# Loads reordered on one queue, and the first tile's multiplies divided differently: a dense expert dispatch on one core

## The chip, the cores and the metric

The kernel runs on one core of a Trainium2 chip. The metric is the device time of one execution in microseconds (us), median of three runs. The profile is of one further execution, taken by the hardware profiler; its times count from the first instruction of the kernel, so its span is somewhat shorter than the device time.

The engines that occur here are VectorE (DVE in the profile), ScalarE (ACT), SyncE (SP, which here only issues transfers) and the core's 16 DMA engines, which move data between HBM and the on-chip memory. "SPq" and "ACTq" are the instruction queues of SP and ACT, from which transfers are issued.

## The reference

For each of 2048 tokens, eight gate weights are normalized by their sum, and the token's 512 values are multiplied by each of the eight:

```python
def setup_inputs():
    batch, seq_len, d_model, n_experts = 8, 256, 512, 8
    # x: (8, 256, 512) float32, gate_weights: (8, 256, 8) float32
def reference(x, gate_weights):
    gate_weights = gate_weights / (np.sum(gate_weights, axis=-1, keepdims=True) + 1e-8)
    output = x[:, :, None, :] * gate_weights[:, :, :, None]
    return output.astype(np.float32)          # (8, 256, 8, 512)
```

4.2 MB of x and 64 KB of gates are read, and 33.6 MB are written.

## The kernel before

The 2048 tokens are laid on 128 partitions with 16 tokens each. Below, "token j" means the j-th token of every partition: one step that handles token j handles 128 tokens of the batch. Its output, eight experts by 512 values, is 4096 values for each partition.

All inputs are loaded by three transfers, which are moved ahead of the barrier at the kernel's entry, so that they are issued first of all. x is loaded in two parts, `HEAD` = 4 tokens and then the other twelve, from SP's queue; the gates from ACT's queue.

```python
SLOTS = 10
HEAD = 4
CHUNKS = ((0, 2, 0), (2, 3, 2), (5, 3, 5), (8, 4, 0), (12, 4, 6))   # first token, tokens, first slot
# ...
    g_all = pool.tile([P, J, E], fp32)
    x_all = pool.tile([P, J, D], fp32)
    ring = pool.tile([P, SLOTS, E, D], fp32)
# ...
    first_load = nc.sync.dma_start(out=x_all[:, 0:HEAD, :], in_=x_v[:, 0:HEAD, :])
    gate_load = nc.scalar.dma_start(out=g_all, in_=g_v)
    last_load = nc.sync.dma_start(out=x_all[:, HEAD:J, :], in_=x_v[:, HEAD:J, :])
    issue_before_entry_barrier(nc, [first_load, gate_load, last_load])

    nc.vector.memset(warm, 0.0)
    nc.scalar.copy(out=warm, in_=warm)          # brings ACT's table load forward
```

Then VectorE normalizes all gates in four operations (lines 74 to 77):

```python
    nc.vector.reduce_sum(out=gsum, in_=g_all, axis=mybir.AxisListType.X)
    nc.vector.tensor_scalar_add(out=gsum, in0=gsum, scalar1=1e-8)
    nc.vector.reciprocal(out=gsum, in_=gsum)
    nc.vector.tensor_tensor(
        out=gn, in0=g_all, in1=gsum.to_broadcast([P, J, E]), op=mult
    )
```

The output is made in a ring of ten slots, one slot for each token. There are two forms of the multiply: a small one, for one token and one expert (512 values for each partition), on ACT (line 84) or VectorE (line 86), and a broadcast one on VectorE, which makes all eight experts of a token in one operation (line 89):

```python
    def scale_one(engine, j, e, slot):
        o_ap, s_ap = ring[:, slot, e, :], gn[:, j, e : e + 1]
        if engine is nc.scalar:
            nc.scalar.mul(out=o_ap, in_=x_all[:, j, :], mul=s_ap)
        else:
            nc.vector.tensor_scalar_mul(out=o_ap, in0=x_all[:, j, :], scalar1=s_ap)

    def scale_token(j, slot):
        nc.vector.tensor_tensor(
            out=ring[:, slot, :, :],
            in0=x_all[:, j : j + 1, :].to_broadcast([P, E, D]),
            in1=gn[:, j, :].unsqueeze(2).to_broadcast([P, E, D]),
            op=mult,
        )
```

Five chunks of 2, 3, 3, 4 and 4 tokens are made and stored by one transfer each, from SP's queue. A chunk and its part of the ring are called a tile below; the first tile is tokens 0 and 1. Each of these two tokens has three small multiplies on ACT and five on VectorE.

```python
    for j0, m, s0 in CHUNKS:
        for i in range(m):
            j, slot = j0 + i, s0 + i
            if j < 2:
                for e in range(E):
                    on_act = e < 3
                    scale_one(nc.scalar if on_act else nc.vector, j, e, slot)
            elif j == 2:
                for e in range(E):
                    scale_one(nc.scalar, j, e, slot)
            elif j == 3:
                for e in range(E):
                    scale_one(nc.scalar if e < 2 else nc.vector, j, e, slot)
            elif i == 0:
                for e in range(E):
                    scale_one(nc.scalar, j, e, slot)
            else:
                scale_token(j, slot)
        nc.sync.dma_start(
            out=out_v[:, j0 : j0 + m, :, :], in_=ring[:, s0 : s0 + m, :, :]
        )
```

The fourth and fifth chunks use slots again, so their multiplies wait until earlier stores have read them.

Of the kernel before, what the change touches and what calls it, by code (L numbers as in the profile page):

```python
# [1 line left out]

# [4 lines left out]

SLOTS = 10
HEAD = 4
CHUNKS = ((0, 2, 0), (2, 3, 2), (5, 3, 5), (8, 4, 0), (12, 4, 6))  # L10


def issue_before_entry_barrier(nc, loads):
    names = [bi.ins.name for bi in loads]

    def move(nc):
        blocks = nc.main_func.blocks
        entry = blocks[0].instructions
        moved = []
        for block in blocks[1:]:  # L20
            for ins in list(block.instructions):
                if ins.name in names:
                    block.instructions.remove(ins)
                    moved.append(ins)
        assert sorted(i.name for i in moved) == sorted(names)
        for ins in reversed(moved):
            at = next(k for k, other in enumerate(entry) if other.engine == ins.engine)
            entry.insert(at, ins)

    nc.at_finalize(move)  # L30


@with_exitstack
def kernel(
    ctx: ExitStack,
    tc: tile.TileContext,
    x: bass.AP,
    gate_weights: bass.AP,
    out: bass.AP,
):  # L40
    nc = tc.nc
    P = 128

    B, S, D = x.shape
    E = gate_weights.shape[-1]
    J = B * S // P

    fp32 = mybir.dt.float32
    mult = mybir.AluOpType.mult

    x_v = x.flatten_outer_dims().rearrange("(p j) d -> p j d", p=P)
    g_v = gate_weights.flatten_outer_dims().rearrange("(p j) e -> p j e", p=P)
    out_v = out.rearrange("b s e d -> (b s) e d").rearrange(
        "(p j) e d -> p j e d", p=P
    )

    pool = ctx.enter_context(tc.tile_pool(name="pool", bufs=1))
# [4 lines that stand above are left out]
    gsum = pool.tile([P, J, 1], fp32)  # L62
    gn = pool.tile([P, J, E], fp32)
    warm = pool.tile([P, 1], fp32)

    first_load = nc.sync.dma_start(out=x_all[:, 0:HEAD, :], in_=x_v[:, 0:HEAD, :])
    gate_load = nc.scalar.dma_start(out=g_all, in_=g_v)
    last_load = nc.sync.dma_start(out=x_all[:, HEAD:J, :], in_=x_v[:, HEAD:J, :])
    issue_before_entry_barrier(nc, [first_load, gate_load, last_load])

    nc.vector.memset(warm, 0.0)  # L71
    nc.scalar.copy(out=warm, in_=warm)  # L72
# [23 lines that stand above are left out]
    for j0, m, s0 in CHUNKS:  # L96
        for i in range(m):
            j, slot = j0 + i, s0 + i
            if j < 2:
                for e in range(E):  # L100
                    on_act = e < 3
                    scale_one(nc.scalar if on_act else nc.vector, j, e, slot)
            elif j == 2:
                for e in range(E):
                    scale_one(nc.scalar, j, e, slot)
# [13 lines that stand above are left out]
# [1 line left out]
_INS = ['x', 'gate_weights']  # L120
_OUTS = [((8, 256, 8, 512), 'float32')]


# [23 lines left out]
```

## Time and profile before

| | us |
|---|---|
| device time, median of three runs (lowest, highest) | 92.21 (92.19, 92.32) |
| span of the profiled execution | 90.4 |
| VectorE busy | 46.6 |
| ScalarE busy | 26.3 |
| gates: issue, landing | 0.12, 5.13 |
| first four tokens of x: issue, issue to landing | 0.00, 4.9 |
| other twelve tokens of x: issue, issue to landing | 0.43, 11.8 |
| first multiply on ACT and on VectorE | 6.30 |
| first store issued | 10.44 |
| last store issued | 56.08 |

A transfer has two times in the profile: the issuing instruction's (some 0.4 us on SP's or ACT's queue) and the landing, when its completion reaches the engine that waits for it. Between them lies the work of the 16 DMA engines, which is shown as their mean busy share and as packets by queue: q1 is SP's queue, q10 ACT's. Mean durations of operations that follow each other on one engine overlap a little: a small multiply on VectorE is listed with 484 ns, and ten of them in a row end 4.06 us after the first begins.

### The profile page before, as it was taken

The page shows a single profiled execution, that of the slowest core. Times are in us where ns is not written, and L with a number is a line of the kernel's source. Part 1 is how long each engine was busy: PE and PEld are TensorE (multiplying, and loading weights), DVE is VectorE, ACT ScalarE, POOL GpSimd, SP SyncE. Part 2 cuts the span into 40 slices and gives each one's busy share as a digit, 9 for nine tenths or more (in the row PEclk, how much of TensorE's full clock was granted, in tenths as well). Part 3 has the DMA queues.
Part 4 walks back from the last instruction along what each step waited for, and adds up shares of the span by engine and source line. Part 5 has one row for each costly group of instructions (what it writes and reads, how often), then busy time and mean ns, then how long its engine had stood idle before and what let it go on. Part 6 is the DMA issues. An engine that isn't in the chain of part 4 may idle for free.

```text
span 90.4 us, 139 instructions
## 1 busy us (share of the span) xinstructions
DVE 46.6 (52%) x30; ACT 26.3 (29%) x42; POOL 0.2 (0%) x4
## 2 busy tenths in 40 slices
DVE  0069999999999999999990495000000000000000
ACT  4229999995990000000000497000000000000000
POOL 0000000000000000000000000000000000000000
DMA  5989899998998899888988999999999994799990
GB/s 145 511 359 511 359 464 464 464 464 348 478 565 348 348 413 630 348 348 370 674 348 348 464 464 464 464 464 464 464 464 464 464 406 203 319 464 464 464 464 0
DMA packets 1152, 37.81 MB, mean 418 GB/s; under 512 B 128, under 2 KB 256, under 8 KB 256
## 3 DMA queue, kind: packets, MB, share of 16 engines
q1 hardware_dynamic: 1008, 37.75, 97.0%
q10 hardware_dynamic: 144, 0.07, 0.3%
HBM read 4.26 MB, written 33.55 MB: 418 GB/s over the span
## 4 chain that ended last, share of the span: by engine, by line
DMA 46%; ACT 9%; DVE 6%; ACTq 1%; issue 0%; SPq 0%
DMA out_dram<-ring 41%; ACT ring L84 9%; DMA g_all<-in_gate_weights_dram 6%; DVE ring L86 4%; ACTq L142 1%; DVE gn L77 0%; DVE gsum L74 0%; DVE gsum L76 0%; DVE gsum L75 0%; ACTq L84 0%; SPq L114 0%
## 5 line engine op out<-in xcount | busy, mean ns | idle before, releaser
L89 DVE TENSOR_TENSOR ring<-x_all,gn 128x4096 f32<-128x4096 f32 x9 | 39.2, 4426 | 3.6 <-DMA out_dram<-ring 3.6
L84 ACT ACTIVATE ring<-x_all,gn 128x512 f32<-128x512 f32 x40 | 24.8, 708 | 28.5 <-DMA out_dram<-ring 24.9
L86 DVE TENSOR_SCALAR ring<-x_all,gn 128x512 f32<-128x512 f32 x16 | 6.4, 484 | 0.0
L74 DVE TENSOR_REDUCE gsum<-g_all 128x16 f32<-128x128 f32 x1 | 0.3, 286 | 3.8 <-DMA g_all<-in_gate_weights_dram 3.8
L72 ACT ACT_TABLE_LOAD x1 | 1.3, 1283 | 1.3 <-PEq L131 1.3
L71 DVE MEMSET warm<- 128x1 f32 x1 | 0.1, 59 | 1.3 <-PEq L131 1.3
L77 DVE TENSOR_TENSOR gn<-g_all,gsum 128x128 f32<-128x128 f32 x1 | 0.3, 291 | 0.0
L76 DVE RECIPROCAL gsum<-gsum 128x16 f32<-128x16 f32 x1 | 0.3, 253 | 0.0
L72 ACT COPY warm<-warm 128x1 f32<-128x1 f32 x1 | 0.2, 192 | 0.0
L75 DVE TENSOR_SCALAR gsum<-gsum 128x16 f32<-128x16 f32 x1 | 0.2, 174 | 0.0
L131 POOL MEMSET const-bfloat16-1.0<- 128x1 bf16 x1 | 0.1, 102 | 0.0
L131 POOL MEMSET const-uint8-127<- 128x1 uint8 x1 | 0.1, 102 | 0.0
L131 POOL MEMSET const-float32-0.0<- 128x1 f32 x1 | 0.1, 98 | 0.2 <-issue 0.2
L131 POOL MEMSET const-float32-1.0<- 128x1 f32 x1 | 0.1, 98 | 0.0
## 6 DMA issues: line engine op xcount, KB each, us to landing
out_dram<-ring SPq DMA_DIRECT2D x2, 6144.0 KB, 22.2
out_dram<-ring SPq DMA_DIRECT2D x1, 4096.0 KB, 11.5
x_all<-in_x_dram SPq DMA_DIRECT2D x1, 3072.0 KB, 11.8
x_all<-in_x_dram SPq DMA_DIRECT2D x1, 1024.0 KB, 4.9
g_all<-in_gate_weights_dram ACTq DMA_DIRECT2D x1, 64.0 KB, 5.0
out_dram<-ring SPq DMA_DIRECT2D x2, 28.2
```

The source lines that it names most:

```text
L71: nc.vector.memset(warm, 0.0)
L72: nc.scalar.copy(out=warm, in_=warm)
L74: nc.vector.reduce_sum(out=gsum, in_=g_all, axis=mybir.AxisListType.X)
L75: nc.vector.tensor_scalar_add(out=gsum, in0=gsum, scalar1=1e-8)
L76: nc.vector.reciprocal(out=gsum, in_=gsum)
L77: nc.vector.tensor_tensor(out=gn, in0=g_all, in1=gsum.to_broadcast([P, J, E]), op=mult)
L84: nc.scalar.mul(out=o_ap, in_=x_all[:, j, :], mul=s_ap)
L86: nc.vector.tensor_scalar_mul(out=o_ap, in0=x_all[:, j, :], scalar1=s_ap)
L89: nc.vector.tensor_tensor(out=ring[:, slot, :, :], in0=x_all[:, j : j + 1, :].to_broadcast([P, E, D]), in1=gn[:, j, :].unsqueeze(2).to_bro ...
L131: nc = _bacc.Bacc("TRN2", target_bir_lowering=False, num_devices=1)
L142: with _tile.TileContext(nc) as tc:
```

## The change

All three loads go into SP's queue, in the order gates, four tokens of x, twelve tokens of x. ACT's queue issues none. The first tile is divided in another way: token 0 is made on VectorE by one broadcast multiply, and token 1 by eight small ones, five on ACT and three on VectorE. The rest of the kernel is the same.

The order is meant to bring the gates in before x, so that VectorE normalizes them while x is on its way, and the multiplies can begin when x's first part lands. The division of the first tile then gives VectorE one long operation and three small ones where it had ten small ones, and ACT five where it had six.

```diff
-    first_load = nc.sync.dma_start(out=x_all[:, 0:HEAD, :], in_=x_v[:, 0:HEAD, :])
-    gate_load = nc.scalar.dma_start(out=g_all, in_=g_v)
-    last_load = nc.sync.dma_start(out=x_all[:, HEAD:J, :], in_=x_v[:, HEAD:J, :])
-    issue_before_entry_barrier(nc, [first_load, gate_load, last_load])
+    loads = [
+        nc.sync.dma_start(out=g_all, in_=g_v),
+        nc.sync.dma_start(out=x_all[:, 0:HEAD, :], in_=x_v[:, 0:HEAD, :]),
+        nc.sync.dma_start(out=x_all[:, HEAD:J, :], in_=x_v[:, HEAD:J, :]),
+    ]
+    issue_before_entry_barrier(nc, loads)
 ...
-            if j < 2:
+            if j == 0:
+                scale_token(j, slot)
+            elif j == 1:
                 for e in range(E):
-                    on_act = e < 3
-                    scale_one(nc.scalar if on_act else nc.vector, j, e, slot)
+                    scale_one(nc.scalar if e < 5 else nc.vector, j, e, slot)
             elif j == 2:
```

## The prediction

> **What bounds the kernel now.** I read the page from the top: engines, then slices, then DMA queues, then the chain, then the DMA issues. The first two parts say who is full.
>
> ```profile
> DVE 46.6 (52%) x30; ACT 26.3 (29%) x42; POOL 0.2 (0%) x4
> ...
> DMA  5989899998998899888988999999999994799990
> ...
> q1 hardware_dynamic: 1008, 37.75, 97.0%
> q10 hardware_dynamic: 144, 0.07, 0.3%
> ```
>
> No compute engine is near full. The two DMA queues together hold the 16 DMA engines for 97.3% of the span. The slices that read 7 or 8 need a second look, since a packet is put into the slice in which it starts; so I asked for two long stretches.
>
> ```profile
> core 0: us, DVE busy (x) ACT busy (x) POOL busy (x), PEclk, DMA share, GB/s
> 1.00:11.50 10.50, 6.26 (x19) 6.67 (x11) 0.00 (x0) 1.00 1.00 409
> 11.50:88.50 77.00, 40.34 (x13) 19.64 (x32) 0.00 (x0) 1.00 1.01 435
> 88.50:90.40 1.90, 0.00 (x0) 0.00 (x0) 0.00 (x0) 1.00 0.00 0
> ```
>
> The DMA share is 1.00 in both. The packet records in the trace say it more sharply: the first packet starts at 1.02 us, the last ends at 89.18 us, and the packets' durations, summed and divided by 16, are 88.0 us of these 88.2. The one place where a hole could be is the turn from loads to stores. There the first engine to finish its share of x ends at 11.497 us and its first store packet starts at 11.499; the last engine ends at 11.837 and starts at 11.839. No hole. So the kernel is one unbroken DMA stream, 1.02 us of start before it and about 1.2 us of completion behind it. The chain of waits tells another story, and it is the one that the change answers:
>
> ```profile
> 0.12 5.01 DMA g_all<-in_gate_weights_dram
> ...
> 5.16 0.30 DVE gsum L74
> ...
> 6.30 4.06 DVE ring L86 x10
> ...
> 10.44 11.52 DMA out_dram<-ring
> ```
>
> Gates land at 5.13, DVE normalizes them until 6.28, ten small multiplies take until 10.36, the first store is issued at 10.44. It lands 11.5 us later, of which 1 us is issue to first packet (x head: issued 0.00, first packet 1.02) and 9.7 us are its packets (8 per engine of 1.213 us). A store issued at 10.44 can have descriptors ready at about 11.46, and the engines fall free at 11.50. So this chain has just come level with the DMA stream: shortening it alone can gain nothing, and lengthening it costs at once.
>
> [...] the gates' 128 packets, on ACT's queue, start between 2.46 us and 4.54 us, threaded through x's first 128 packets (1.02 to 4.49), so 64 KB take as long as 1 MB. [...] The trace: ten small multiplies start 0.402 us apart, so eight are 3.2 us, against 4.35 us from one broadcast multiply to the next for the same 4096 elements; the broadcast is the dearer form on DVE. [...]
>
> ```profile
> L89 DVE TENSOR_TENSOR ring<-x_all,gn 128x4096 f32<-128x4096 f32 x9 | 39.2, 4426 | 3.6 <-DMA out_dram<-ring 3.6
> L84 ACT ACTIVATE ring<-x_all,gn 128x512 f32<-128x512 f32 x40 | 24.8, 708 | 28.5 <-DMA out_dram<-ring 24.9
> L86 DVE TENSOR_SCALAR ring<-x_all,gn 128x512 f32<-128x512 f32 x16 | 6.4, 484 | 0.0
> ```
>
> **The change part by part.**
>
> *Start of the stream.* SP's two issues start at 0.00 and 0.43; now there are three, at about 0.00 (gates), 0.43 (x head), 0.86 (x rest). SP reaches the barrier about 0.4 us later, so ACT's table load and DVE's memset start near 1.7 instead of 1.3; they end by 3.2, before any data is there. No cost. The gates' first packet comes at 1.02. It now pays what x's first packets paid: the 128 packets of x head took 46.65 us together, 2.92 per engine, while 8 at the later 0.309 would be 2.47. So 0.45 us per engine is ramp. Gates: 1.02 + 0.45 + 8 x 0.027 = about 1.7. x head's descriptors are there at 0.43 + 1.02 = 1.45, before the gates are through, so I expect little or no hole. If the ramp is paid only once, x head ends at 1.7 + 2.47 = 4.17; if it is paid again, at 4.6. Before, its last packet ended at about 4.49. The middle is 4.4, and everything behind it moves alike: the loads' end moves by -0.3 to +0.15. I allow up to +0.3 on the far side, for a hole between the gates and x.
>
> *Gates and normalizing.* Landing lag is 0.4 to 0.6 us behind the last packet (gates before: 4.57 to 5.13; x head: 4.51 to 4.93). So gates land near 2.2, and the four DVE operations, 5.16 to 6.28, end near 3.4. What ends last is now x head: 4.4 + 0.42 = about 4.85. The two engines begin to multiply there, instead of at 6.30: 1.45 us earlier.
>
> *First tile.* DVE now does one broadcast (4.35) and three small ones (2 x 0.402 + 0.484 = 1.29): 5.64 us, against 4.06 for ten small ones, so +1.58. ACT does five, and they start 0.617 apart (24 in 14.82): about 3.2 us, beside DVE and shorter. First tile ready: 4.85 + 0.03 + 5.64 = 10.5, against 10.36. The 1.45 won and the 1.58 spent cancel. First store issued at about 10.6, its descriptors ready at about 11.6; the engines fall free at 11.4 to 11.75. So the hole at the turn is 0 to 0.2 us on the early engines and none on the late ones, and it is the late ones that end the run.
>
> *Later.* The second tile is ready at 17.1 now (DVE's first late broadcast, 12.64 + 4.43) and the stream needs it at about 20 (first store's packets end at 21.2, less 1.02). DVE is at the same place as before when the first tile is done, so this stays at 17.2. The fourth store is issued at 47.49 and the third's packets end near 50.2: 1.7 us of room. All bytes are the same 37.8 MB.
>
> Sum: stream start as before, loads' end between -0.3 and +0.3 with a middle near 0, hole at the turn 0 to 0.2, the rest unchanged. 92.2 + 0 + 0.1 = 92.3 us.
>
> **The rivals.** *A, the chain is right:* one may read the page's fourth part as saying that the gates' 5.01 us and the small multiplies are on the path, and that calculating 1.3 us sooner brings up to 1.3 us: 90.9. For it stands the chain's order of time; against it, that the engines are never idle between 1.02 and 89.18. I give it next to nothing. *B, a smoother start:* the gates take the ramp while x's issue is still on its way, and x head then runs at 0.309 from its first packet; the loads end 0.3 earlier. Only if the first store is as early does this reach the end: DVE then starts at 4.6 and the store is ready at 11.35 against engines free at 11.2. About 92.0. *C, the store comes late:* x head lands at 5.2 or the broadcast is held up, and the first store's descriptors come up to 0.5 us after the engines are free. The stream then has a hole that nothing refills: 92.7. For it stands that the new DVE work is longer by 1.58 and hangs on one landing. *D, a hole at the start:* the engines finish the gates and wait for x's descriptors, and each pays the ramp twice: 0.3 to 0.45 later, 92.5 to 92.65. *E, VectorE becomes the bound:* its busy time rises by 4.43 - 7 x 0.402 = 1.6 us to about 48 of 90, all in the first 11 us. No.
>
> **Range and chances.** B sets the low end and C or D the high one: 91.95 to 92.75. The three runs before lie within 0.13 us, so the repeat noise adds little. 2% is 1.84 us; going below 90.4 would need fewer bytes or faster engines, which nothing here brings, and going above 94.05 would need a hole of 1.8 us. Within 2%: 0.97; slower 0.02, faster 0.01.
>
> **What would show it right or wrong.** In the changed profile: gates landing near 2.2 and the multiplies starting near 4.85 on both engines, at x head's landing (right), or still at the gates (the order in the queue did not help). The first store issued at 10.4 to 10.8. DMA share still 1.00 from 1 to 88.5 us. The chain's early part now x head, one broadcast, three small multiplies. The prediction is wrong if the DMA stream has a hole over 0.4 us at 1.5 or at 11.5, if x head's packets take clearly less than 2.9 us per engine, or if the later stores are no longer queued ahead of need.

## The result, and the profile after

The changed kernel takes 92.73 us (median; 92.62 to 92.80) against 92.26 us for the kernel before beside it: a ratio of 1.0051, with a 95% interval of 1.0038 to 1.0064. It is half a per cent slower, which the prediction put at a tenth of a per cent.

The page of the changed kernel, same parts as shown of before:

```profile
DVE 48.1 (53%) x24; ACT 25.7 (28%) x41; POOL 0.2 (0%) x4
...
DMA  4998999799799779988998999999999559999990
...
q1 hardware_dynamic: 1152, 37.81, 97.1%
```

All packets are on one queue now, and their share is 97.1% of a span longer by 0.54 us: the DMA stream is still nearly all there is. Its two long stretches, in the same columns as before (stretch, its length, busy time of three engines, clock, DMA share, GB/s):

```profile
1.00:11.50 10.50, 6.99 (x11) 7.47 (x12) 0.00 (x0) 1.00 1.01 406
11.50:88.50 77.00, 41.10 (x15) 18.22 (x30) 0.00 (x0) 1.00 1.01 436
```

The change of rate is in the first stretch: 406 GB/s where it was 409. A stretch of three microseconds at the beginning is plainer. First the kernel before, then the changed one:

```profile
1.00:4.00 3.00, 0.06 (x1) 1.48 (x2) 0.00 (x0) 1.00 0.98 346
```

```profile
1.00:4.00 3.00, 1.00 (x5) 1.47 (x2) 0.00 (x0) 1.00 0.88 287
```

A tenth of the DMA engines' time is lost between 1 and 4 us: 0.10 x 3 = 0.3 us. Four of VectorE's five operations in the same stretch are the gain that the change was made for: the gates are normalized at 2.91 us, where it was 6.26. The chain of waits shows what that gain meets, with start, duration and what it is (of the nine small multiplies in its last line, the first three belong to the first tile):

```profile
0.00 0.38 SPq L67
0.38 0.05 issue
0.43 4.98 DMA x_all<-in_x_dram
...
5.51 4.42 DVE ring L91
9.94 3.56 DVE ring L88 x9
```

x's first part is issued at 0.43 instead of 0.00 and lands at 5.41 instead of 4.93. The multiplies begin at 5.50 and the first store is issued at 11.21 instead of 10.44:

```profile
11.21 15.71 SPq L117 DMA_DIRECT2D out_dram<-ring  x3
```

The packet records give the same story for the DMA engines, in us. They carry no engine number: two packets are put to one engine where the second starts within a few ns of the end of the first, and the 128 packets of each load and of the first store fall in this way into 16 rows of eight, one for each engine. The engines begin and end a transfer at different times; the first and last are given. The last column is the end of the stream.

| | x's first packet | x rest's packets begin | x rest's packets end | first store's packets begin | last packet ends |
|---|---|---|---|---|---|
| before | 1.02 | 4.23 to 4.57 | 11.50 to 11.84 | 11.50 to 11.84 | 89.18 |
| after | 1.48 | 4.46 to 5.09 | 11.73 to 12.36 | 12.05 to 12.37 | 89.83 |

Of the 0.65 us by which the last packet is later in these two profiled executions (the medians differ by 0.47), 0.53 (11.84 to 12.36) are there when the slowest engine ends its share of x, and they were there when it began x's second part (4.57 to 5.09). That engine has no hole before the first store; the first ones to finish wait until 12.05 (0.07 us in the mean over all 16). The other 0.12 us are gathered by the stores, whose packets take a little longer (median 1.820 us instead of 1.815 for 48 KB).

So the question was no longer whether the DMA stream is the bound, but what the two parts of the change do to it: the order of loads at its start, the division of the first tile at the turn from loads to stores. My theory was that the order costs all of it, because x is issued behind the gates; the rival was that the longer first tile and its late store cost it.

### The profile page after: what moved, and what is told of

Same layout as the page of the kernel before. It is cut to its first block, busy times and chain, and to the rows that moved or that the text cites. A ratio compares the mean times of both kernels' runs of the same rounds, so it can differ in the third digit from the quotient of the medians.

```text
span 91.0 us, 132 instructions
## 1 busy us (share of the span) xinstructions
DVE 48.1 (53%) x24; ACT 25.7 (28%) x41; POOL 0.2 (0%) x4
## 3 DMA queue, kind: packets, MB, share of 16 engines
q1 hardware_dynamic: 1152, 37.81, 97.1%
## 4 chain that ended last, share of the span: by engine, by line
DMA 33%; DVE 23%; ACT 5%; ACTq 1%; SPq 0%; issue 0%; DVEq 0%
DMA out_dram<-ring 27%; DVE ring L91 19%; DMA x_all<-in_x_dram 5%; ACT ring L86 5%; DVE ring L88 4%; ACTq L145 1%; SPq L67 0%; DVEq L91 0%; ACTq L86 0%; SPq L117 0%
## 5 line engine op out<-in xcount | busy, mean ns | idle before, releaser
L91 DVE TENSOR_TENSOR ring<-x_all,gn 128x4096 f32<-128x4096 f32 x10 | 43.6, 4414 | 6.0 <-DMA out_dram<-ring 3.4
L86 ACT ACTIVATE ring<-x_all,gn 128x512 f32<-128x512 f32 x39 | 24.2, 709 | 29.1 <-DMA out_dram<-ring 26.8
L88 DVE TENSOR_SCALAR ring<-x_all,gn 128x512 f32<-128x512 f32 x9 | 3.6, 476 | 0.0
## 6 DMA issues: line engine op xcount, KB each, us to landing
x_all<-in_x_dram SPq DMA_DIRECT2D x1, 3072.0 KB, 11.8
```

What stands on the lines that cost most here:

```text
L91: nc.vector.tensor_tensor(out=ring[:, slot, :, :], in0=x_all[:, j : j + 1, :].to_broadcast([P, E, D]), in1=gn[:, j, :].unsqueeze(2).to_bro ...
```

## The two parts alone

**e1_order_only**: the new order of loads, the first tile as before.

```diff
-            if j == 0:
-                scale_token(j, slot)
-            elif j == 1:
+            if j < 2:
                 for e in range(E):
-                    scale_one(nc.scalar if e < 5 else nc.vector, j, e, slot)
+                    on_act = e < 3
+                    scale_one(nc.scalar if on_act else nc.vector, j, e, slot)
```

> The new order of loads with the first tile divided as before. Theory (the start): the loss of 0.47 us is made at the start, where x's first packets begin at 1.48 us instead of 1.02 us because x is issued 0.43 us later and the gates' packets fill only half of that. Then this kernel loses as much as the changed one: 92.6 to 92.75 us, x's first packets at about 1.48, first store issued near 9.7, no hole at the turn from loads to stores. Rival (the turn): the loss comes from the longer first tile, whose store is issued at 11.21 instead of 10.44. Then this kernel is back at 92.2 to 92.3 us.

Measured: 93.37 us, ratio 1.0125 (1.0111 to 1.0139). Neither theory had this: with a first tile that is ready 1.58 us sooner the kernel is slower than the changed one by 0.64 us. The store is issued at 9.63 as expected, and there is no hole. But x itself comes later. The transfers of this kernel (size, median us from issue to landing):

```profile
out_dram<-ring SPq DMA_DIRECT2D x1, 4096.0 KB, 13.6
x_all<-in_x_dram SPq DMA_DIRECT2D x1, 3072.0 KB, 12.6
```

and of the changed one:

```profile
out_dram<-ring SPq DMA_DIRECT2D x1, 4096.0 KB, 11.2
x_all<-in_x_dram SPq DMA_DIRECT2D x1, 3072.0 KB, 11.8
```

x's second part, issued at about 0.9 us in both, needs 0.8 us longer. In the packet records its 24 KB packets run at 0.912 us each from 5.1 us on, as in the kernel before, until one that starts at 10.50; from there to the last, at 11.72, a dozen take between 0.98 and 1.43 us. The engines end x at 11.75 to 13.15 us, spread over 1.4 us instead of 0.6, and they stay out of step: their last packets end between 89.20 and 90.47. In the table above each engine has eight of a load's 128 packets, however late it is; here too the slowest one's last packet, at 90.47, ends the stream.

**e2_split_only**: the loads as before, the first tile divided in the new way.

```diff
-    loads = [
-        nc.sync.dma_start(out=g_all, in_=g_v),
-        nc.sync.dma_start(out=x_all[:, 0:HEAD, :], in_=x_v[:, 0:HEAD, :]),
-        nc.sync.dma_start(out=x_all[:, HEAD:J, :], in_=x_v[:, HEAD:J, :]),
-    ]
+    first_load = nc.sync.dma_start(out=x_all[:, 0:HEAD, :], in_=x_v[:, 0:HEAD, :])
+    gate_load = nc.scalar.dma_start(out=g_all, in_=g_v)
+    last_load = nc.sync.dma_start(out=x_all[:, HEAD:J, :], in_=x_v[:, HEAD:J, :])
```

> The loads as before, the first tile divided in the new way. Both theories agree that the multiplies start at 6.30 us as before and the first store is issued near 12.0 us. With 0.84 us from issue to first packet (seen in the changed kernel: 11.21 to 12.05) and the DMA engines free at 11.50 to 11.84 us, the stream has a hole of 1.0 to 1.35 us at the turn. If a hole in the stream goes into the time in full: 93.2 to 93.6 us. Rival (the stores have slack that takes it up): 92.3 to 92.7 us.

Measured: 93.61 us, ratio 1.0154 (1.0140 to 1.0168). The store is issued at 12.23. Between 9.5 and 13 us the DMA share shows the hole, first before, then this kernel:

```profile
9.50:13.00 3.50, 3.50 (x10) 3.50 (x6) 0.00 (x0) 1.00 1.20 515
```

```profile
9.50:13.00 3.50, 3.50 (x7) 3.50 (x7) 0.00 (x0) 1.00 0.52 225
```

The packets of x end between 11.44 and 12.13, the first store's begin at 13.07 and later; the holes are 1.4 us in the mean, the last engine begins its stores at 13.22 instead of 11.84, and the time rises by 1.43. Here the hole goes into the time in full. So each part alone costs more than both together: order +1.2 us, division +1.4, both +0.5. They don't add because each moves the first store, in opposite directions (to 9.63 and 12.23).

## A store can also come too early

The new theory was that a store issued so early that its packets could start while the engines still load x slows these loads. (The expectations speak of its descriptors; the profile shows none, only the lag from a store's issue to its first packet, 0.84 us in the changed kernel, 11.21 to 12.05.) In e1 the slow packets begin 0.87 us after the store's issue, close to that lag. To test it, VectorE was given useless small multiplies ahead of the first tile in e1; they write a ring slot that is made much later, so they do nothing but delay the store.

```diff
+    for k in range(2):      # 3 and 5 in the other two kernels
+        nc.vector.tensor_scalar_mul(
+            out=ring[:, 9, k, :], in0=x_all[:, 0, :], scalar1=gn[:, 0, 0:1]
+        )
+
     for j0, m, s0 in CHUNKS:
```

**e5_delay2**

> The order-only kernel (93.37 us) with two more small multiplies on VectorE ahead of the first tile; they write part of a ring slot that is made much later, so nothing of the output changes. Theory (early store): a store whose descriptors reach the DMA engines while they still load x slows those loads and takes the engines out of step; order-only loses 0.64 us to the changed kernel in this way, because its first store is issued at 9.63 us and x's packets end at 11.7 to 13.1. Then 0.8 us later is better although VectorE has more to do: issue near 10.43, time 92.8 to 93.1 us. Rival (the form): ten small multiplies beside the loads cost in themselves, or the loads were slowed by something else than the store: 93.3 to 93.5 us.

**e5_delay3**

> As before with three added small multiplies: first store issued near 10.84 us, descriptors there near 11.7, when the first engines are through with x. Theory (early store): no slow packets of x and no hole, only the loss at the start is left: 92.6 to 92.75 us. Rival (the form): 93.3 to 93.5 us.

**e5_delay5**

> As before with five added: first store issued near 11.64 us, descriptors there near 12.5, and the engines free at 11.7 to 12.4 have a hole of 0.1 to 0.75 us. Theory (early store): the time has its lowest point between, so this one is slower again than with three: 93.0 to 93.2 us. Rival (the form): 93.4 us or more, with no lowest point.

Measured, with the kernels of the same order of loads put by the time of their first store:

| kernel | first store issued, us | x rest's packets end, us | median, us | ratio to before (95% interval) |
|---|---|---|---|---|
| e1_order_only | 9.63 | 11.75 to 13.15 | 93.37 | 1.0125 (1.0111 to 1.0139) |
| e5_delay2 | 10.43 | 11.75 to 12.34 | 92.73 | 1.0053 (1.0040 to 1.0065) |
| e5_delay3 | 10.81 | 11.79 to 12.35 | 92.59 | 1.0050 (1.0035 to 1.0066) |
| the changed kernel | 11.21 | 11.73 to 12.36 | 92.73 | 1.0051 (1.0038 to 1.0064) |
| e5_delay5 | 11.76 | 11.77 to 12.53 | 93.14 | 1.0100 (1.0086 to 1.0115) |

Adding 0.8 us of useless work to VectorE makes the kernel 0.64 us faster. The kernels with two and three came out a little below what the theory expected, and the one with five within it. The late packets of x are all 0.912 us again in e5_delay2 and e5_delay3. With five, the hole is back (0.6 us in the mean), and so is the loss. The rival, that ten small multiplies cost in themselves, is out: all three have them. Here is the same transfer of x in e5_delay3, 11.8 again:

```profile
out_dram<-ring SPq DMA_DIRECT2D x1, 4096.0 KB, 11.6
x_all<-in_x_dram SPq DMA_DIRECT2D x1, 3072.0 KB, 11.8
```

**e6_half_tile** tries the early store in the kernel before, whose loads are untouched.

```diff
-CHUNKS = ((0, 2, 0), (2, 3, 2), (5, 3, 5), (8, 4, 0), (12, 4, 6))
+CHUNKS = ((0, 1, 0), (1, 1, 1), (2, 3, 2), (5, 3, 5), (8, 4, 0), (12, 4, 6))
```

> The kernel before with its first tile stored in two halves of one token, the loads untouched: the first half's store is issued near 8.4 us, its descriptors there near 9.3, 2.2 us before the engines are through with x. Theory (early store): x's late packets grow beyond 912 ns, the engines end x at different times, and the time rises by 0.5 us or more: 92.7 to 93.4 us, without any change of the loads' order. Rival (loads and stores don't disturb each other within one queue): 92.2 to 92.35 us, the little above coming from 256 packets of 16 KB in place of 128 of 32 KB.

Measured: 93.33 us, ratio 1.0117 (1.0103 to 1.0131). The first half's store is issued at 8.55, and x's second part takes 12.8 us to land instead of 11.8:

```profile
out_dram<-ring SPq DMA_DIRECT2D x2, 2048.0 KB, 11.0
x_all<-in_x_dram SPq DMA_DIRECT2D x1, 3072.0 KB, 12.8
```

All 16 KB store packets take 0.611 us, so they are not the loss. Nearly all packets of x that start from 9.64 on, two for each engine, take 1.0 to 1.65 us instead of 0.912; together 0.82 us for each engine. So the slow packets come with the store's early issue, not with the order of the loads, which here is that of the kernel before.

**e8_after_act6** takes the changed kernel and moves one small multiply from VectorE to ACT, so that its store comes 0.4 us sooner.

```diff
-                    scale_one(nc.scalar if e < 5 else nc.vector, j, e, slot)
+                    scale_one(nc.scalar if e < 6 else nc.vector, j, e, slot)
```

> The changed kernel with six small multiplies of token 1 on ACT and two on VectorE: first store issued near 10.8 us instead of 11.21. Theory: the hole at the turn goes and the engines don't fall into step, so the part of the loss that belongs to the late store goes and that of the start stays: 92.5 to 92.65 us, as with three added multiplies (92.59). Rival (the turn costs nothing at 11.21): 92.7 to 92.8 us.

Measured: 92.73 us, ratio 1.0053 (1.0041 to 1.0065), the same as the changed kernel; the theory failed and its rival held. The store is issued at 10.75, no engine waits, and no packet of the stores is long. But the slowest engine ends x at 12.28, against 12.36, and it never had a hole. The late store of the changed kernel costs nothing that can be measured: its hole (0.07 us in the mean) lies on engines that would have finished ahead of the slowest.

## The start

What is left of the changed kernel's loss, 0.5%, is common to every kernel that issues the gates ahead of x from SP's queue. Four kernels look into it.

**e4_gates_twice**: one more load of the gates ahead of all.

```diff
+    g_spare = pool.tile([P, J, E], fp32)
 ...
     loads = [
+        nc.sync.dma_start(out=g_spare, in_=g_v),
         nc.sync.dma_start(out=g_all, in_=g_v),
```

> The changed kernel with one more load of the gates ahead of all, into a tile that nothing reads. Theory (the start): each small load ahead of x costs one issue of 0.43 us, whatever its bytes: x's first packets at about 1.9 us and 93.1 to 93.2 us. Rival (bytes): the 128 packets of 27 ns over 16 engines are 0.22 us, so 92.9 to 93.0 us. Rival (a single cost of being second): no change, 92.7 us.

Measured: 93.27 us, ratio 1.0119 (1.0106 to 1.0133), so 0.54 us over the changed kernel and somewhat more than the theory had. x's first packet starts at 1.95. The first small load ahead of x went with 0.47 us (the changed kernel) and the second with 0.54, each more than its 0.22 us of packets (eight of 27 ns for each engine).

**e3_x_from_act**: gates first from SP, x from ACT's queue.

```diff
         nc.sync.dma_start(out=g_all, in_=g_v),
-        nc.sync.dma_start(out=x_all[:, 0:HEAD, :], in_=x_v[:, 0:HEAD, :]),
-        nc.sync.dma_start(out=x_all[:, HEAD:J, :], in_=x_v[:, HEAD:J, :]),
+        nc.scalar.dma_start(out=x_all[:, 0:HEAD, :], in_=x_v[:, 0:HEAD, :]),
+        nc.scalar.dma_start(out=x_all[:, HEAD:J, :], in_=x_v[:, HEAD:J, :]),
```

> The changed kernel, with gates still issued first from SP's queue but both parts of x from ACT's queue, so that x's issue doesn't stand behind the gates' issue. Theory (the start): x's first packets come at 1.1 to 1.2 us, the gates' packets beside them, the early hole is gone and the time is 92.2 to 92.4 us; the gates land near 2 to 3 us. Rival (the gates ahead of x cost the stream in themselves, by a second ramp of the reads or by small packets): the time stays at 92.6 to 92.75 us.

Measured: 92.90 us, ratio 1.0080 (1.0067 to 1.0094). The time missed the expectation, while the start did what the theory said: x's first packet at 1.21, its last end at 11.85 as in the kernel before (11.84), gates landed at 2.04, and the stretch at the start is full again:

```profile
1.00:4.00 3.00, 1.06 (x5) 1.47 (x2) 0.00 (x0) 1.00 0.97 344
```

The loss is now at the turn. Ten of the 16 engines' first store packets take 1.45 to 2.02 us instead of 1.21, and the last packets end between 89.17 and 89.94. The store was issued at 10.71; with the changed kernel's 0.84 us its first packet could have started near 11.55, by estimate. What differs is that the stores follow x on another queue; that this is the cause was not tried apart.

**e7_x0_first_act3** and **e7_x0_first_act4** put token 0 of x ahead of the gates, to cover the gates' issue, and divide token 1 so that the store should come at the right time.

```diff
     loads = [
+        nc.sync.dma_start(out=x_all[:, 0:1, :], in_=x_v[:, 0:1, :]),
         nc.sync.dma_start(out=g_all, in_=g_v),
-        nc.sync.dma_start(out=x_all[:, 0:HEAD, :], in_=x_v[:, 0:HEAD, :]),
+        nc.sync.dma_start(out=x_all[:, 1:HEAD, :], in_=x_v[:, 1:HEAD, :]),
 ...
-                    scale_one(nc.scalar if e < 5 else nc.vector, j, e, slot)
+                    scale_one(nc.scalar if e < 3 else nc.vector, j, e, slot)   # e < 4 in the second
```

> Four loads on SP's queue: token 0 of x, gates, tokens 1 to 3, tokens 4 to 15. Token 0 is made by one broadcast multiply, token 1 by three small ones on ACT and five on VectorE. Now a transfer of 256 KB covers the gates' issue and the gates cover the next one. Theory (start hole): x's first packets come at 1.0 us again, no hole is left at the start, VectorE begins at about 4 us and the first store is issued near 10.6 us, at the late edge of the time in which it neither slows x nor comes late: 92.2 to 92.4 us. Rival (gates ahead of most of x, or a fourth small load, cost in themselves): 92.6 to 92.8 us.

> As the one before with four small multiplies of token 1 on each engine: first store issued near 10.2 us, in the middle of that time. Theory (start hole, and a store at the right moment): 92.2 to 92.3 us, as the kernel before, and no less, since the stream of packets is the bound. Rival: 92.6 us or more.

Measured: 94.03 us, ratio 1.0207 (1.0165 to 1.0249), and 94.70 us, ratio 1.0268 (1.0244 to 1.0293). Both are far worse than either theory had it. The start is emptier than in any other kernel (this is the first of the two):

```profile
1.00:4.00 3.00, 0.86 (x5) 1.48 (x2) 0.00 (x0) 1.00 0.82 242
```

Between 2 and 4 us the engines idle 0.5 us in the mean. In the first kernel, tokens 1 to 3 have their first packet at 2.32 us, which is 1.41 us after their issue, where x head in the changed kernel needed 1.05, and the packets of token 0 (0.97 us for each engine) and of the gates (0.22 in the changed kernel) don't cover that. Why it takes so long is open. The slow beginning of the reads is also paid twice: in the first kernel token 0's 2 KB packets take 0.97 us for each engine where eight at their median of 0.084 would be 0.67, and the 6 KB packets behind the idle time 2.34 where eight at 0.234 would be 1.87. So x ends later, at 12.03 to 13.71 us in the first and 11.78 to 14.94 in the second, while the stores were issued at 10.73 and 10.10, and there are slow packets of x near the end (up to 1.32 and 1.54 us). That looks like early stores again, but it was not tried apart: in both kernels packets of x take up to 1.0 or 1.1 us already between 5 and 8 us, before any store, and in the first the late slow ones begin 0.63 us after the store's issue, sooner than in e1.

**e9_gates_second**: the kernel before with all loads on SP's queue, the gates between the two parts of x.

```diff
-    first_load = nc.sync.dma_start(out=x_all[:, 0:HEAD, :], in_=x_v[:, 0:HEAD, :])
-    gate_load = nc.scalar.dma_start(out=g_all, in_=g_v)
-    last_load = nc.sync.dma_start(out=x_all[:, HEAD:J, :], in_=x_v[:, HEAD:J, :])
+    loads = [
+        nc.sync.dma_start(out=x_all[:, 0:HEAD, :], in_=x_v[:, 0:HEAD, :]),
+        nc.sync.dma_start(out=g_all, in_=g_v),
+        nc.sync.dma_start(out=x_all[:, HEAD:J, :], in_=x_v[:, HEAD:J, :]),
+    ]
```

> The kernel before with all loads on SP's queue in the order x head, gates, x rest, and its own division of the first tile. The gates' and x rest's descriptors are there by about 2 us, long before x head's packets end near 4.2. Theory (issue): the hole of the changed kernel, between the gates' last packet and x's first, comes from x being issued 0.43 us after the gates; then there is no hole here, x's last packet ends at 11.8 to 11.9 and the time is 92.2 to 92.35 us. Rival (short packets): the hole follows any run of 512-byte packets in the same queue, since they are over before the reads behind them bring data; then the engines idle 0.2 to 0.35 us between 4 and 5 us, x ends near 12.1 and the time is 92.45 to 92.65 us. The kernel with token 0 of x ahead of the gates speaks for the rival: its engines idled about 0.3 us there although 256 KB stood ahead.

Measured: 92.26 us beside 92.23 for the kernel before, ratio 1.0005 (0.9988 to 1.0021). The gates land at 5.11 and the store is issued at 10.41, both as before, and the stretch at the start is full:

```profile
1.00:4.00 3.00, 0.06 (x1) 1.47 (x2) 0.00 (x0) 1.00 0.99 344
4.00:5.00 1.00, 0.00 (x0) 0.00 (x0) 0.00 (x0) 1.00 1.18 474
```

Behind the gates' packets the engines idle 0.01 us in the mean in the packet records. Eleven of its 14 runs lie between 92.07 and 92.34 us; the other three took 92.84, 92.89 and 93.84, while none of 19 runs of the kernel before was above 92.51, and what delayed these three is open. In its usual runs, then, no cost was measured for a row of 512-byte packets behind x's first part, nor for a single queue. In the changed kernel the gates stood at the head of the queue and were through at 1.2 to 1.43 us, before x's first packet at 1.48; there the engines had a hole of 0.26 us in the mean, and the kernel took 0.47 us longer. No version found here beats the kernel before.

## Why the prediction was right, and where it was off

That the time hardly changes was right, and for the reason given. The size was not: 92.73 us lies 0.02 us inside the upper end of the range of 91.95 to 92.75, an end that the rivals C and D had set, and 0.4 us above the expected 92.3. Falling inside owes more to luck than to the sum: rival D, half of which came true, had been put at 92.5 to 92.65. Of the signs named, the stores stayed queued ahead of need and x's landing released the multiplies, but these began at 5.50 instead of 4.85, and the first store was issued at 11.21 instead of 10.4 to 10.8.

- **The stream of packets is the bound, and the chain through the gates is not**: right. The gates land 3.4 us sooner and nothing comes of it; e2 shows a hole of 1.4 us going into the time as 1.43.
- **Start of the stream**: wrong in size, and this is the term that puts the middle 0.4 us too low. I had the gates take the ramp that x's first packets paid (gates through at 1.7, x's descriptors at 1.45, so "little or no hole"), and the loads' end moved by -0.3 to +0.3 with a middle near 0. In fact the gates' packets took 25 to 58 ns each from the first on and were through at 1.2 to 1.43, before x's first packet at 1.48; and x paid its ramp in full, as before (3.02 us for each engine, 2.92 before). The hole between the gates and x is 0.26 us in the mean over the engines. The slowest engine's x ended 0.53 us later. That is half of rival D, "a hole at the start", which I had at 92.5 to 92.65: the hole came, but the ramp was not paid twice, since the gates paid none. The sum was also off in itself: it set 4.17 (ramp paid once) and 4.6 (paid twice), both for an engine that starts at 1.02 with the mean ramp, against 4.49, the end of the slowest engine before. By the same sum the kernel before has 1.02 + 2.92 + 0.22 = 4.16, so like for like the change is 0 with one ramp and +0.45 with two, not -0.3 and +0.15. Measured, x's second part begins 0.41 us later in the mean (4.37 to 4.78), of which the hole is 0.26 and x's longer ramp 0.1.
- **Gates and normalizing**: landing near 2.2 was 1.77, normalized near 3.4 was 2.91: right in kind, and off by the same ramp that the gates didn't pay.
- **First tile**: 5.64 us of VectorE was 5.61 (5.51 to 11.12), since the sum took the trace's own durations: 4.35 us for one broadcast (they start 4.33 to 4.34 apart) and 0.402 for a small multiply (they start 0.395 to 0.401 apart). Its beginning was put at 4.85 and was 5.50, since x head landed late; so the store was at 11.21 and not at 10.6.
- **Hole at the turn**: 0 to 0.2 us on early engines, none on late ones, and the late ones end the run: right, with 0.07 in the mean and none on the slowest; e8 shows that removing it brings nothing. x and the store both came about 0.6 us later than predicted, since both hang on x's first part, and so the turn looked as foretold. One term was mis-sized: 1.02 us from a store's issue to its first packet, taken from x's first load, is 0.84 in the changed kernel (11.21 to 12.05). So the first store of the kernel before had perhaps not "just come level" with the DMA engines: by an estimate with 0.84 its packets could have started near 11.28, some 0.2 us before the first engine fell free at 11.50.
- **"Shortening it alone can gain nothing, and lengthening it costs at once"**: half right. Lengthening costs (e2). But shortening the chain is not free: by a store that comes too soon e6 loses 1.1 us, and e1 0.64 us more than the changed kernel. The prediction had no term for that, and without it the change would look like two losses; the longer first tile is what keeps the new order from costing 1.2 us.

Three things stay open: by what mechanism a waiting store slows loads on their way, why the loads of the kernels with token 0 ahead began so late, and why the first store packets are slow when x comes from the other queue (e3).

## What to carry to other kernels

Where the DMA engines are hardly idle, as here (97.1% of the span), look first at the stream: at its first packet, at the turn from loads to stores, and at the slowest of the 16 engines, not at the chain that happens to lead to the first store. Be wary of a small load at the head of the queue on which a large one follows: here it went with 0.47 us (the changed kernel), and a second one with 0.54 more (e4); behind the first large part it was free in most runs (e9, 92.26 us against 92.23). And time the first store for the end of the loads: here, with both on one queue, an issue 1.2 to 1.9 us ahead of the moment at which the slowest engine ends its loads was right (changed kernel 12.36 - 11.21, e5_delay2 12.34 - 10.43), while 0.8 us ahead (e5_delay5) cost 0.4 us more and 0.8 us sooner than the earliest right one (e1) 0.6 us more.

## What was not expected of the hardware

- A store issued well before the loads ended (9.63 us in e1, 8.55 in e6) went with slower loads at their end: 24 KB packets of x that started 0.87 us (e1) or 1.09 us (e6) after the store's issue, or later, took up to 1.43 and 1.65 us instead of 0.912. In e1 the 16 engines were then 1.4 us apart, and still 1.3 us at the end of the kernel: what an engine had lost early it did not get back.
- Where engines had to wait for the first store (the changed kernel, e2, e5_delay5), store packets take a little longer until the end: median 1.820 us for 48 KB and 2.422 for 64 KB. Where the store waited for them (before, e8, e9), these are 1.815 and 2.418. Waiting alone does not explain it, and the cause stays open: e4 has the longer packets too, and its engines waited 0.01 us in the mean.
- The gates' small packets at the very head of the stream took 27 ns each in the median (512 bytes; 25 to 58), as they did among x's packets in the kernel before (median 27), while x's 8 KB packets right behind them started slowly, up to 1.22 us instead of 0.309: in this kernel the ramp came with the large reads, not with being first. x's second part, which follows without a hole in the kernel before and in e9, shows no ramp there: all its packets take 0.912 us.
